# First-stage modulation of a two-layer diffusion trunk: a quarter of the columns to each column group of TensorE, instead of a quarter of the rows

## The chip, the cores and the metric

The kernel runs on one core of a Trainium2 chip. The metric is the device time of one execution in microseconds (us); the median of three runs before the change is 1126.43 us (1126.07 to 1126.88).

## What is computed

The reference is a trunk of two layers (DEPTH 2) over 256 latent and 256 context tokens of width 2048. Each layer first makes a shift, a scale and a gate from the conditioning vectors c and c_ctx, normalises the tokens, and multiplies the modulated tokens by a wide input matrix:

```
shift, scale, gate = split(silu(c) @ w_mod[l] + b_mod[l], 3)
shift_c, scale_c, gate_c = split(silu(c_ctx) @ w_mod[l] + b_mod[l], 3)
h   = rmsnorm(x,   g_pre[l]) * (1 + scale)   + shift
h_c = rmsnorm(ctx, g_pre[l]) * (1 + scale_c) + shift_c
proj = h @ w_in[l];  proj_c = h_c @ w_in[l]
```

Behind that come a gated position-mixing branch (columns a_u, a_v, a_g), windowed attention, a Fourier branch, and the output projection. The change touches only the making of shift and scale in layer 0.

## The kernel before, in words

Tokens lie transposed: 16 tiles `yo[k]` of 128 features by 512 tokens (256 latent, 256 context). All products with `w_in` and `w_out` are done on TensorE (PE) with each operand split into a high and a low part, three products per block: high by high, high by low, low by high. `hh[k]` and `hl[k]` are the two parts of tile k of the modulated input; `whi` and `wlo` those of the weights, made by ScalarE (ACT, the cast, L513) and VectorE (DVE, the subtraction, L515).

**The first stage** (the branch `if l == 0` of `layer`, L783 to L914) is a loop over the 16 feature tiles k, because the modulation of tile k+1 is finished only while tile k is being multiplied. In pass k of the loop, from k = 3 on, the order of PE is written by hand:

- `first_av` with (0,0) and (0,1): for four token blocks the products of `hh[k]` with the high and the low part of the a_v weights, 8 matmuls of 512 columns (L771, tile `ps_av`).
- `m.rounds()`: the modulation products of tile k+1 (L182, tile `ps_mod`). The weights of a tile are 16 row blocks (kk) of 128 rows by 256 columns (128 scale, 128 shift) in f32. The stationary operand is `cpad[:, kk]`, 128 by 32, of which two columns (c and c_ctx) are not zero. Row block kk goes to column group kk mod 4 of the array, so that each group of 32 output rows holds the sum over a quarter of the rows, for all 256 columns.
- `first_av` with (1,0): the products of `hl[k]`, 4 matmuls of 512 columns ("the low part").
- `m.cols()`: the second step. DVE has turned the 128 by 256 sums in blocks of 32 by 32 (`turn`, L188); four small matmuls with the 0/1 matrix `selq` (L194, tile `ps_modc`) add up the four column groups and put the result on the features' partitions.
- `start_au`: the products for three heads of a_u, 9 matmuls of 512 columns (L545 to L547, tile `ps_au`).

Each f32 matmul of the modulation is two instructions on PE, each with its own weight load. ACT turns the result of the second step into `gs` and `sh` (`mod_k`, L202, L203; for the first tiles DVE does, L205, L207), and `make_h1` makes the next tile: `hh[k+1]` by two ACT instructions of 256 columns (L663), the full-precision value by two more, then `hl[k+1]` by DVE (L665, `low_part`).

Two sets are special. Tile 10 (`Aside`) and the pair of tiles 14 and 15 (`AsidePair`, 512 columns at once) are summed in part on DVE (L231, L233): pieces of their weights are multiplied and added up in the passes that `SUMMED` lists (for the pair passes 9 to 12), at most `SLOT[k]` of these instructions between the turn of pass k and `low_part` (8 in passes 7, 8 and 12). PE multiplies only the rest of their row blocks and the two DVE sums (L242).

In this stage DVE, ACT and the queue of SyncE (SP), which issues the weight loads, run in the order in which the code is written. After it only PE does; DVE, ACT and SP are ordered by a scheduler at build time. The loads of a set go to fixed buffers, which are free once the set before last has been multiplied (`Mod.load`, L166 to L175). `splits(n)` emits the next cast and subtraction of `w_in` weights.

Of the kernel before, what the change touches and what calls it, by code (L numbers as in the profile page):

```python
# [13 lines left out]
P = 128  # L14
# [52 lines left out]
def trunk_kernel(ctx: ExitStack, tc: tile.TileContext, xT, xhalf, cT, wss, wsl, wmod, win, wout0, wout1, const, vec, rows,  # L67
# [91 lines left out]
    class Mod:  # L159
# [17 lines left out]
        def rounds(self, n=4):  # L177
            if self.ps is None:
                self.ps = ms_ps("mod")
            for kg in range(self.done, self.done + n):  # L180
                for kk in range(4):
                    PE.matmul(self.ps[32 * kk:32 * kk + 32, 0:self.N], cpad[:, kg * 4 + kk], self.w[kg * 4 + kk],  # L182
                              start=kg == 0, stop=kg == 3, tile_position=(0, 32 * kk))
            self.done += n

        def turn(self):
            self.r = w2k([P, self.N])
            V.transpose(self.r, self.ps[:, 0:self.N])  # L188

        def cols(self):  # L190
            ps = ms_ps("modc")
            rv = self.r.rearrange("p (j q c) -> p j q c", q=4, c=32)
            for q in range(4):
                PE.matmul(ps[32 * q:32 * q + 32, 0:4], cc("selq"), rv[:, :, q, 0:2], start=True, stop=True,  # L194
                          tile_position=(0, 32 * q))
            mod_k(self.k, ps[:, 0:4].rearrange("p (j s) -> p j s", s=2))

    def mod_k(k, v):

# [9 lines left out]
    class Aside(Mod):  # L209
# [25 lines left out]
        def rounds(self, n=4):  # L235
            n = 2 * sum(SUMMED[self.k].values())
            self.ps = ms_ps("mod")
            todo = [(cpad[:, kk], self.weights(kk)) for kk in range(n, KT)]
            todo += [(unit[:, s], self.sums(s)) for s in range(2)]
            for i, (st, mv) in enumerate(todo):  # L240
                c = slice(32 * (i % 4), 32 * (i % 4) + 32)
                PE.matmul(self.ps[c, 0:self.N], st, mv, start=i < 4, stop=i >= len(todo) - 4,  # L242
                          tile_position=(0, 32 * (i % 4)))

        def weights(self, kk):
            return self.w[kk // 2][:, kk % 2]
# [4 lines left out]
    class AsidePair(Aside):  # L251
# [17 lines left out]
            return self.acc[s]  # L269

        def cols(self):
            ps = ms_ps("modc")
            rv = self.r.rearrange("p (j q c) -> p j q c", q=4, c=32)
            for q in range(4):
                PE.matmul(ps[32 * q:32 * q + 32, 0:8], cc("selq"), rv[:, :, q, 0:2], start=True, stop=True,
                          tile_position=(0, 32 * q))
            v = ps[:, 0:8].rearrange("p (j k s) -> p j k s", k=2, s=2)
            mod_k(self.k, v[:, :, 0])
            self.second = lambda: mod_k(self.k + 1, v[:, :, 1])

# [443 lines left out]
    def layer(l):  # L724
# [58 lines left out]
        if l == 0:  # L783
            mod = {}
            for k in range(KT):
                def splits(n):
                    for _ in range(n):
                        W.emit()

                def next_h():  # L790
                    if k + 1 < KT:
                        if k < XAHEAD:
                            make_h0(k + 1)
                        else:
                            return make_h1(k + 1)
                    return lambda: None

                if k % 2 == 0:
                    take(k)
                if k == 0:  # L800
                    W.load()
                if k + 1 < KT and k + 1 not in (*LOADED, *(j + 1 for j in PAIRS)):
                    mod[k + 1] = Mod(k + 1)
                    mod[k + 1].load()
                if k < 2:
                    W.load_rest()
                for j, at in LOADED.items():
                    if j in PAIRS:
                        for _ in range(LOADS[k]):
                            W.load()  # L810
                    if k == min(at):
                        mod[j] = AsidePair(j) if j in PAIRS else Aside(j, "ctrh")
                    for _ in range(at.get(k, 0)):
                        mod[j].load_piece()

                def beside():
                    for j, at in SUMMED.items():
                        i = sum(at[i] for i in at if i < k)
                        for i in range(i, i + at.get(k, 0)):
                            yield from mod[j].steps(i)  # L820

                ops = beside()

                def aside(n):
                    for _ in range(n):
                        next(ops, None)

                m = mod.get(k + 1)
                if k == 0:
                    first_av(0, range(4), ((0, 0),))  # L830
                    first_av(0, range(4), ((0, 1),))
                    m.rounds(2)
                    first_av(0, range(4), ((1, 0),))
                    m.rounds(1)
                    e = W.emitting(512)
                    next(e)
                    next(e)
                    take(0, (1,))
                    m.rounds(1)
                    m.turn()  # L840
                    first_au(0, ((0, 0),))
                    next(state["e0"])
                    m.cols()
                    list(state["e0"])
                    first_au(0, ((0, 1),))
                    next_h()
                    state["e1"] = e
                elif k == 1:
                    first_au(0, ((1, 0),))
                    first_av(1, range(4), ((0, 0), (0, 1)))  # L850
                    m.rounds()
                    m.turn()
                    first_av(1, range(4), ((1, 0),))
                    m.cols()
                    e = W.emitting(512)
                    next(e)
                    start_au(1, (0, 1))
                    make_h0(2, e)
                    list(state["e1"])
                    list(e)  # L860
                    scale_x(3, rb0)
                elif k == 2:
                    first_av(2, range(4), ((0, 0),))
                    first_av(2, range(4), ((0, 1),))
                    first_av(2, range(4), ((1, 0),))
                    m.rounds()
                    m.turn()
                    start_au(2, (0,))
                    e = W.emitting(512)
                    next(e)  # L870
                    next(e)
                    m.cols()
                    start_au(2, (1,))
                    low_part = next_h()
                    scale_x(4, rb0)
                    scale_x(5, rb0)
                    low_part()
                    list(e)
                    ws_[2] = W.next()
                    for i in range(k + 1):  # L880
                        start_au(i, (2,))
                else:
                    pair = k + 1 in PAIRS
                    first_av(k, range(nt), ((0, 0), (0, 1)))
                    if m:
                        m.rounds()
                        m.turn()
                    if k < KT - 2:
                        splits(min(SPLITS[k], 1))
                    first_av(k, range(nt), ((1, 0),))  # L890
                    if m:
                        m.cols()
                    low_part = next_h()
                    if pair:
                        m.second()
                    aside(SLOT.get(k, 0))
                    for i in XSCALE.get(k, ()):
                        scale_x(i, rb0)
                    low_part()
                    if k == 4:  # L900
                        for i in (14, 15):
                            scale_x(i, rb0)
                    splits(SPLITS[k] if k >= KT - 2 else max(SPLITS[k] - 1, 0))
                    if k == KT - 2:
                        first_stage.close()
                    list(ops)
                    if k == KT - 3:
                        A.activation(sb([P, 4], F32, "es", 2), zero4, AF.Gelu_apprx_tanh)
                    if k >= KT - 2:
                        for _ in range(2):  # L910
                            with low(LAG), tc.issue_after(W.last.ins):
                                next(mods)
                    take(k, (1, 2))
                    start_au(k)  # L914
# [521 lines left out]
    with tc.manual_schedule(engines={EN.PE}):  # L1436
# [43 lines left out]
                PE.matmul(rb[:, j * P:(j + 1) * P], r0[:, j:j + 1].to_broadcast([P, P]), ident, start=True, stop=True)  # L1480

        m.rounds(1)
        m.turn()
        spread(0)
        scale_x(0, rb, LAT)
        m.cols()
        spread(1)
        rb0 = sb([P, T], F32, "acc")
        e = W.emitting(512)
        next(e)  # L1490
# [87 lines left out]
```

## Time and profile before

| | |
|---|---|
| median of 3 runs | 1126.43 us (1126.07 to 1126.88) |
| the profiled execution | 1126.57 us, of which the span from first to last instruction is 1124.8 us |
| PE busy | 1116.0 us, 99% of the span |
| DVE busy | 919.9 us, 82% |
| ACT busy | 548.8 us, 49% |
| loads on SP's queue | 229.79 MB |
| TensorE clock granted | 0.999 |

The profile is one execution, recorded on the chip. A matmul's end in it is modelled, so that a busy PE is not PE at its peak; what PE loses shows in the starts of its instructions. The chain of work is followed back from the last instruction: at each step to what released it, or to the instruction before it on its engine. PEld are the weight loads of PE, which can run beside its matmuls. In the lines of the timeline, the two numbers ahead are the start from the span's beginning and the length, in us; "x8" means that eight instructions of one kind are drawn together.

### The profile page before, as it was taken

Reading aid. Unit: us, or ns where it says so; the run is one execution under the profiler, and the core shown is the slowest. Engines: PE = TensorE matmul, PEld = TensorE weight load, DVE = VectorE, ACT = ScalarE, POOL = GpSimd, SP = SyncE. Lnnn points to the kernel's source line nnn. Section 1 sums busy time; section 2 is a strip of 40 time slices with the busy share of each in tenths; the row PEclk is TensorE's granted clock in tenths of the full one; section 3 lists DMA queues with packets and bytes.
Section 4 is the critical chain, followed back from the end, with each engine's and each line's share of the span. In section 5 each row is a group of like instructions: output and inputs, shape, how many; then the busy total and the mean of one; then the engine's idle time right before and its main releaser. Section 6 shows DMA issues by size and latency. Waiting matters only on the chain.

```text
span 1124.8 us, 16564 instructions
## 1 busy us (share of the span) xinstructions
PE 1116.0 (99%) x6069; PEld 919.4 (82%) x6072; DVE 919.9 (82%) x1573; ACT 548.8 (49%) x1044; POOL 34.9 (3%) x44
## 2 busy tenths in 40 slices
PE   8999999999999999999999999999999999999998
PEld 3666788888888888888888888988888888898886
DVE  2667699899988897988998989396989689878883
ACT  5454723322335667632533334266665369867551
POOL 0000000000000000000000000030500000000000
PEclk9999999999999999999999999999999999999999
DMA  9999755576655343465566665285946686456872
GB/s 360 402 401 399 258 165 173 168 241 206 212 189 182 112 152 121 128 202 186 169 194 206 218 207 186 95 197 193 236 154 204 211 294 198 159 180 200 302 254 75
DMA packets 76002, 235.84 MB, mean 210 GB/s; under 512 B 8704, under 2 KB 13200, under 8 KB 75920
## 3 DMA queue, kind: packets, MB, share of 16 engines
q1 hardware_dynamic: 71136, 229.79, 60.7%
q0 software_dynamic: 4064, 3.69, 2.2%
q10 hardware_dynamic: 720, 1.31, 0.3%
q8 instruction: 47, 0.77, 0.3%
q14 instruction: 35, 0.29, 0.1%
HBM read 232.65 MB, written 2.10 MB: 209 GB/s over the span
## 4 chain that ended last, share of the span: by engine, by line
PE 88%; DVE 5%; DMA 3%; ACT 2%; issue 1%; ACTq 0%; POOLq 0%; DVEq 0%; SPq 0%
PE ps_t L545 14%; PE ps_t L547 14%; PE ps_t L546 14%; PE ps_t L692 9%; PE ps_t L693 5%; PE ps_av L771 4%; PE ps_v L1174 3%; PE ps_y L545 3%; PE ps_y L547 3%; PE ps_y L546 3%; PE ps_mod L182 2%; DVE macc L294 2%; DVE wlo L515 1%; PE ps_v L1175 1%; PE ps_tp L1116 1%; DMA mraw<-in_wmod_dram 1%
## 5 line engine op out<-in xcount | busy, mean ns | idle before, releaser
L513 ACT CAST whi<-raw 128x1024 fp32r<-128x1024 f32 (+1 forms) x209 | 215.9, 1037 | 314.7 <-PE ps_t L546 214.0
L545 PE MATMUL ps_t<-hh,whi 128*128 128x512 f32 (+1 forms) x752 | 290.7, 387 | 0.0
L515 DVE TENSOR_TENSOR wlo<-raw,whi 128x1024 fp32r<-128x1024 f32 (+1 forms) x209 | 250.4, 1202 | 48.3 <-ACT whi L513 40.5
L546 PE MATMUL ps_t<-hl,whi 128*128 128x512 f32 (+1 forms) x752 | 289.6, 385 | 0.0
L547 PE MATMUL ps_t<-hh,wlo 128*128 128x512 f32 (+1 forms) x752 | 289.4, 385 | 0.0
L294 DVE SCALAR_TENSOR_TENSOR macc<-mraw,cs,macc 128x512 f32<-128x512 f32 x360 | 250.5, 744 | 14.6 <-DMA mraw<-in_wmod_dram 14.1
L692 PE MATMUL ps_t<-hh,whi 128*128 128x512 f32 x512 | 184.6, 399 | 0.0
L547 PEld LDWEIGHTS ps_t<-hh,wlo 128*128 128x128 f32 x752 | 141.3, 188 | 28.7
L545 PEld LDWEIGHTS ps_t<-hh,whi 128*128 128x128 f32 x752 | 141.3, 188 | 26.7
L546 PEld LDWEIGHTS ps_t<-hl,whi 128*128 128x128 f32 x752 | 141.3, 188 | 26.3
L693 PE MATMUL ps_t<-hh,wlo 128*128 128x256 f32 x512 | 143.4, 280 | 0.0
L692 PEld LDWEIGHTS ps_t<-hh,whi 128*128 128x128 f32 x512 | 96.1, 188 | 21.2
L693 PEld LDWEIGHTS ps_t<-hh,wlo 128*128 128x128 f32 x512 | 96.7, 189 | 0.4
L545 PE MATMUL ps_y<-whi,hh 128*128 128x512 f32 x104 | 41.3, 397 | 0.0
L547 PE MATMUL ps_y<-whi,hh 128*128 128x512 f32 x104 | 40.6, 391 | 0.0
L546 PE MATMUL ps_y<-wlo,hh 128*128 128x512 f32 x104 | 40.5, 389 | 0.0
L562 ACT CAST w2k<-ps_tp 128x512 fp32r<-128x512 f32 x40 | 23.4, 584 | 21.2 <-PE ps_scc L546 13.7
L575 POOL TENSOR_TENSOR rs_b<-rs_a,mhalf 128x2 f32<-128x2 f32 (+1 forms) x6 | 6.7, 1115 | 759.5 <-DVE mx L1366 584.6
L563 DVE TENSOR_TENSOR w2k<-ps_tp,w2k 128x512 fp32r<-128x512 f32 x40 | 27.4, 684 | 3.5 <-ACT w2k L562 2.3
L1096 ACT ACTIVATE w2k<-w2k,den 128x512 f32<-128x512 f32 (+1 forms) x48 | 28.1, 647 | 0.7 <-DVE den L1091 0.6
L188 DVE STREAM_TRANSPOSE w2k<-ps_mod 128x256 f32<-128x256 f32 (+1 forms) x15 | 7.0, 468 | 26.1 <-PE ps_mod L182 24.5
L771 PE MATMUL ps_av<-whi,hh 128*128 128x512 f32 x64 | 24.6, 397 | 0.0
(483 smaller groups left out, 1819.3 us busy)
## 6 DMA issues: line engine op xcount, KB each, us to landing
raw<-in_win_dram SPq DMA_DIRECT2D x158, 512.0 KB, 4.1
mraw<-in_wmod_dram SPq DMA_DIRECT2D x128, 512.0 KB, 4.4
raw<-in_wout_dram SPq DMA_DIRECT2D x60, 512.0 KB, 4.5
mraw<-in_wsl_dram SPq DMA_DIRECT2D x12, 512.0 KB, 7.3
mg<-in_wsl_dram SPq DMA_DIRECT2D x7, 512.0 KB, 9.0
mgl<-in_wsl_dram SPq DMA_DIRECT2D x7, 512.0 KB, 9.0
yo<-in_xhalf_dram POOLq DMA_DIRECT2D x28, 128.0 KB, 7.2
yo<-in_xT_dram SPq DMA_DIRECT2D x12, 256.0 KB, 4.9
```

Of the source, the lines that this page charges most:

```text
L294: V.scalar_tensor_tensor(out=acc[:, s], in0=w[:, kk % 2], scalar=c, in1=acc[:, s], op0=ALU.mult, op1=ALU.add)
L513: A.copy(ph, rc)
L515: self.last = V.tensor_tensor(out=pl, in0=rc, in1=ph.bitcast(F32), op=ALU.subtract)
L545: PE.matmul(ps, st[0], mv[0], start=start, stop=False)
L546: PE.matmul(ps, st[0], mv[1], start=False, stop=False)
L547: PE.matmul(ps, st[1], mv[0], start=False, stop=stop)
L563: V.tensor_tensor(out=lo, in0=src, in1=hi.bitcast(F32), op=ALU.subtract)
L692: PE.matmul(ps, w[0], h, start=k == 0, stop=False)
L693: PE.matmul(ps[:, 0:S], w[1], h[:, 0:S], start=False, stop=k == KT - 1)
L771: PE.matmul(ps, st[a], mv[b], start=start and (a, b) == (0, 0), stop=stop and (a, b) == (1, 0))
L1096: A.activation(prob[i][:, b * w:(b + 1) * w], prob[i][:, b * w:(b + 1) * w], AF.Copy, scale=den[:, c:c + 1])
L1174: PE.matmul(vps[t], hi, wk, start=k == 0, stop=False)
```

## The change

Column group q of the array now takes a quarter of the columns over all 16 row blocks. For each row block the same stationary operand is loaded into all four groups, and each group multiplies 64 columns: two runs of 32 (one of scale, one of shift). The sums are then complete, and the turn of the 128 by 64 result (128 by 128 for the pair) puts them on the features' partitions. The second step with `selq` is gone; `mod_k` reads the turned tile in SBUF instead of PSUM. In passes k >= 3 the modulation's products and the turn stand behind the low part of a_v, so that the subtraction of `splits` stands ahead of the turn in DVE's order. Ahead of the loop, the two halves of `spread` (the broadcast of the first norm's factors) stand together ahead of the turn, and the second step's matmuls no longer stand between them.

```diff
@@ class Mod
             for kg in range(self.done, self.done + n):
-                for kk in range(4):
-                    PE.matmul(self.ps[32 * kk:32 * kk + 32, 0:self.N], cpad[:, kg * 4 + kk], self.w[kg * 4 + kk],
-                              start=kg == 0, stop=kg == 3, tile_position=(0, 32 * kk))
+                for kk in range(4 * kg, 4 * kg + 4):
+                    self.row(cpad[:, kk], self.w[kk], kk == 0, kk == KT - 1)
             self.done += n
 
+        def row(self, st, mv, start, stop):
+            mv = mv.rearrange("p (j q c) -> p j q c", q=4, c=32)
+            for q in range(4):
+                PE.matmul(self.ps[32 * q:32 * q + 32, 0:self.N // 4], st, mv[:, :, q], start=start, stop=stop,
+                          tile_position=(0, 32 * q))
+
         def turn(self):
-            self.r = w2k([P, self.N])
-            V.transpose(self.r, self.ps[:, 0:self.N])
+            self.r = w2k([P, self.N // 4])
+            V.transpose(self.r, self.ps[:, 0:self.N // 4])
 
         def cols(self):
-            ps = ms_ps("modc")
-            rv = self.r.rearrange("p (j q c) -> p j q c", q=4, c=32)
-            for q in range(4):
-                PE.matmul(ps[32 * q:32 * q + 32, 0:4], cc("selq"), rv[:, :, q, 0:2], start=True, stop=True,
-                          tile_position=(0, 32 * q))
-            mod_k(self.k, ps[:, 0:4].rearrange("p (j s) -> p j s", s=2))
+            mod_k(self.k, self.r.rearrange("p (j c) -> p j c", c=32)[:, :, 0:2])
@@ class Aside, rounds (the same in AsidePair.cols: no matmuls, r read directly)
             for i, (st, mv) in enumerate(todo):
-                c = slice(32 * (i % 4), 32 * (i % 4) + 32)
-                PE.matmul(self.ps[c, 0:self.N], st, mv, start=i < 4, stop=i >= len(todo) - 4,
-                          tile_position=(0, 32 * (i % 4)))
+                self.row(st, mv, i == 0, i == len(todo) - 1)
@@ layer, passes k >= 3
                     first_av(k, range(nt), ((0, 0), (0, 1)))
-                    if m:
-                        m.rounds()
-                        m.turn()
                     if k < KT - 2:
                         splits(min(SPLITS[k], 1))
                     first_av(k, range(nt), ((1, 0),))
                     if m:
+                        m.rounds()
+                        m.turn()
                         m.cols()
@@ ahead of layer(0)
         m.rounds(1)
+        spread(0)
+        spread(1)
         m.turn()
-        spread(0)
+        m.cols()
         scale_x(0, rb, LAT)
-        m.cols()
-        spread(1)
```

More of the change, by code (lines that the diff above doesn't have):

```diff
@@ L271, in cols @@
         def cols(self):
[L272 to L277, printed above, removed]
+            v = self.r.rearrange("p (j k c) -> p j k c", k=2, c=32)[:, :, :, 0:2]
             mod_k(self.k, v[:, :, 0])
```

## The prediction, made before the changed kernel ran

> **What bounds the kernel now.** I read the page first, then the busy time by stage, then the chain of work through the first stage.
>
> ```profile
> PE 1116.0 (99%) x6069; PEld 919.4 (82%) x6072; DVE 919.9 (82%) x1573; ACT 548.8 (49%) x1044; POOL 34.9 (3%) x44
> ...
> DMA  9999755576655343465566665285946686456872
> ...
> q8 instruction: 47, 0.77, 0.3%
> ```
>
> PE is busy 99% of the span, and the DMA engines are full in the first four of the 40 slices (112 us), not later. The view of busy time by stage, for passes 3, 12 and 13 of the first stage (pass 13 multiplies the pair):
>
> ```profile
> 45.81:53.07 7.26, 7.26 (x62) 4.88 (x62) 4.64 (x8) 3.53 (x8) 0.00 (x0) 1.00 1.03 398
> ...
> 109.95:117.22 7.27, 7.27 (x63) 4.88 (x62) 6.12 (x10) 3.53 (x8) 0.00 (x0) 1.00 1.05 392
> 117.22:124.50 7.28, 7.28 (x47) 4.39 (x46) 4.63 (x7) 3.53 (x8) 0.00 (x0) 1.00 0.62 233
> ```
>
> A pass takes 7.27 us, all of it PE. (The columns are PE, PEld, DVE, ACT and POOL with their instructions, then PE's clock, the DMA engines' share and GB/s.) Two others are close behind: the loads, with a share of 1.03 to 1.05, and in pass 12 DVE with 6.12 us. The chain of work through passes 12 and 13:
>
> ```profile
> 109.95 1.82 PE ps_av L771 x8
> 111.77 1.86 PE ps_mod L182 x32
> 113.63 1.13 PE ps_av L771 x4
> 114.76 0.17 PE ps_modc L194 x8
> 114.94 0.43 PE ps_au L545
> 115.36 0.23 PE ps_au L546
> ...
> 117.22 1.82 PE ps_av L771 x8
> 119.04 1.85 PE ps_mod L242 x16
> ...
> 122.04 0.18 PE ps_modc L275 x8
> 122.22 0.43 PE ps_au L545
> ...
> 124.50 0.70 PE ps_av L771 x3
> ```
>
> No gap: in the first stage the end is set by PE's program, and what PE saves there counts as long as loads, ACT and DVE keep up. A matmul of 512 columns costs 0.23; the first behind a change of the array's division costs 0.43.
>
> **The change, step by step.** *The second step goes.* 0.17 us, and since the low part now follows the high part without a change between, its four cost 4 x 0.23 = 0.93 instead of 1.13. That is 0.37 us a pass. What hid the turn's latency was the low part; what is late next is weighed below.
>
> *The products.* 32 instructions of 256 columns become 128 of 64, each with its own weight load. The timeline of pass 3:
>
> ```profile
> 48.44 0.61 PE L182 MATMUL ps_mod<-macc,kt 128*32 128x256 f32 x8
> 48.87 0.61 PE L182 MATMUL ps_mod<-vv,kt 128*32 128x256 f32 x8
> 49.42 1.20 PE L771 MATMUL ps_av<-whi,hl 128*128 128x512 f32 x4
> 50.54 0.24 PE L194 MATMUL ps_modc<-w2k,cst 128*32 128x4 f32 x8
> 50.72 0.50 PE L545 MATMUL ps_au<-hh,whi 128*128 128x512 f32 x1
> ```
>
> Eight start within 48.87 - 48.44 = 0.43 us: four groups at once, 0.215 us a round. A quarter of the columns is 0.054 a round, and 32 rounds give the same 1.72 as 8 rounds before. So the columns cost nothing more; the question is whether PE starts 256 instructions (loads counted) in that time, 7 ns each. The nearest row: the 16 of the second step (8 loads, 8 matmuls of four columns, where columns cost next to nothing) take 50.72 - 50.54 = 0.18 us, 11 ns each, and that with the change of division in it. The ends are thus +0 and 256 x 11 ns = 2.8 us, +0.95 on 1.86. Less than +0 is excluded, the columns being the same. I take +0.09, near the lower end, since in the rows above weight loads run beside matmuls without lengthening a round.
>
> [...]
>
> A full pass then gives 0.37 - 0.09 = 0.28 us.
>
> *The way from the products to `hh[k+1]`.* It is now covered by a_u alone: 0.43 + 8 x 0.23 = 2.3 us. ACT in pass 4, then DVE:
>
> ```profile
> 58.12 0.35 ACT L202 ACTIVATE gs<-ps_modc,gg,vecs 128x2 f32<-128x2 f32 x1 [3.70 <-PE ps_modc L194]
> 58.66 1.09 ACT L663 ACTIVATE hh<-yo,sh,gs 128x256 fp32r<-128x256 f32 x2
> 59.66 1.08 ACT L663 ACTIVATE w2k<-yo,sh,gs 128x256 f32<-128x256 f32 x2
> ```
> ```profile
> 49.55 0.45 DVE L188 STREAM_TRANSPOSE w2k<-ps_mod 128x256 f32<-128x256 f32 x1 [2.62 <-PE ps_mod L182]
> ...
> 60.78 0.69 DVE L665 TENSOR_TENSOR hl<-w2k,hh 128x512 fp32r<-128x512 f32 x1 [1.10 <-ACT w2k L663]
> ...
> 80.10 1.66 DVE L233 SCALAR_TENSOR_TENSOR ctrh<-kt,cs,ctrh 128x256 f32<-128x256 f32 x4
> ...
> 83.26 0.69 DVE L665 TENSOR_TENSOR hl<-w2k,hh 128x512 fp32r<-128x512 f32 x1
> ...
> 113.70 0.45 DVE L188 STREAM_TRANSPOSE w2k<-ps_mod 128x256 f32<-128x256 f32 x1 [0.48 <-PE ps_mod L182]
> 114.07 0.71 DVE L233 SCALAR_TENSOR_TENSOR nstrh<-yo,cs,nstrh 128x512 f32<-128x512 f32 x1
> ...
> 119.34 0.69 DVE L665 TENSOR_TENSOR hl<-w2k,hh 128x512 fp32r<-128x512 f32 x1
> ...
> 121.04 0.72 DVE L188 STREAM_TRANSPOSE w2k<-ps_mod 128x512 f32<-128x512 f32 x1 [1.02 <-PE ps_mod L242]
> ```
>
> Call E the end of the last product (48.87 + 0.61 = 49.48 in pass 3). The turn starts at E + 0.07. 256 columns take 0.45 and 512 take 0.72, so 64 take about 0.25: done at E + 0.32. `gs` starts 0.04 later, `hh` 0.54 behind it (58.12 to 58.66), its first half is there at E + 1.5. PE wants it at E + 2.1. Hidden, with 0.6 to spare; that also covers `mod_k`, whose reading from SBUF no row shows (its rows from PSUM are 0.35 and 0.25, and half as much more would not be seen).
>
> *The low part comes 1.9 us earlier in a pass*, and it needs `hl`. In before the products stood ahead of it. PE asks for `hl[k+1]` at E + 2.1 + 8 x 0.23 = E + 4.0. By ACT's rows it is ready at E + 0.36 + (61.47 - 58.12) = E + 3.7: just in time. But where DVE has its sums between turn and `hl`, they decide. Passes 7 and 8: eight sums of 0.395 (80.10 to 83.26), ready at E + 0.07 + 0.19 + 3.16 + 0.69 = E + 4.1; with the 0.1 to 0.2 that a stop of PE costs, 0.3 each. **Pass 12**: eight sums of 0.66 (114.07 to 119.34), so E + 0.07 + 0.19 + 5.27 + 0.69 = E + 6.2 against E + 4.0. PE stands 2.2 us, 2.3 with the restart, ahead of the low part of pass 13. Before, the pair's products filled that time (119.04 + 1.85 = 120.9, `hl` there at 120.03). The pair's products, which wait for the same sums, now come behind low part and all: passes 12 and 13 together take 14.55 - 2 x 0.28 + 2.3 = 16.3 us.
>
> *Loads.* SP issues as the DMA engines take them, 400 GB/s throughout:
>
> ```profile
> DMA packets 14663, 39.21 MB, mean 400 GB/s; under 512 B 1628, under 2 KB 1628, under 8 KB 14653
> ```
> ```profile
> L174 SPq DMA_DIRECT2D yo<-in_wsl_dram x4: 328/328/328, 74.5 to 77.7; - x4
> ...
> DMA to landing us min/median/max: 7.2/7.5/8.4
> ```
> ```profile
> 83.95 1.86 PE ps_mod L182 x32
> ```
>
> They don't get faster. The last weights of pass 8 land at 77.7 + 7.2 = 84.9; PE's products there end at 83.95 + 1.86 = 85.8, and the quarter that needs these weights begins some 0.6 before, at 85.2. The products now stand 0.9 us later in the pass and take their row blocks in order, which gives 0.3 more: PE may come 1.5 us earlier (1.8 with the stop ahead of it) and no more. Buffers come free 0.9 us later, against 7 us between issue and landing: no effect on the rate.
>
> *The start and the rest.* In passes 0 to 2 the loads set the pace, and only the second steps of passes 1 and 2 count, less 0.2 for `hh[2]`, which ACT makes behind a cast that waits for its load: 0.55. Pass 3 loses 0.1, since the subtraction, late there for the same reason, is now ahead of the turn.
>
> **The sum**, against the profiled 1126.57: start 0.55; passes 3 to 8, 10 and 11, eight x 0.28 = 2.24; pass 9 (a short set) 0.35; less 0.1, less 0.6; gives 2.44 gained at pass 12. Passes 12 and 13 lose 16.3 - 14.55 = 1.75. Left: 0.7, so 1125.9. Behind the stage I count nothing: PE runs there without gaps in a fixed order. The scheduler may order DVE and ACT otherwise; the trace has no price for it, and 0.5 is my choice for the likeliest value, against the gain, since an order with no gaps can only get some: 1126.4.
>
> **The rivals.**
>
> *Starts of instructions set the pace* (slower). Beyond 7 ns each nanosecond costs 0.26 us a set, 2.8 us in eleven sets, so that it decides from 8 ns on. At 11 ns a set takes 2.8 us and a pass loses 0.57 instead of gaining 0.28: eight passes 4.6; the start 0.8 (two sets of 0.85 more, 0.4 of it beside waits for loads, less the 0.55); pass 9 nothing; stops 0.7; passes 12 and 13 1.75 + 0.85: +8.7, 1135. For it: the 11 ns. Against: that row has a change of division in it. [...]
>
> *Late code blocks* (slower). PE's 6069 + 6072 instructions came in 47 packets of the instruction queue, 258 to a packet of 16 KB. A pass had 62 + 62 (row of pass 3) and now has 124 - 64 - 16 + 256 = 300, so a block is used up in 6 us, and when it falls on the products alone, in under 3. A fetch must pass DMA engines that are full, where data takes 7 us to land. Two or three late ones of 1 us: 1129.
> [...]
>
> *`hl` isn't late* (faster). If the pass-12 stop doesn't come, the whole 2.44 + 0.6 + 0.56 stands, cut by the loads to 1.5 at pass 8 and then 0.28 + 0.35 + 4 x 0.28, about 3.2: 1123.3. Against: DVE's order is written out, and its rows are plain.
>
> **How the numbers follow.** Forecast, 1126.4 with its own range 1124.8 to 1128: 0.58. Starts: 0.18. Code blocks: 0.16. `hl` in time: 0.08. A measurement tells 0.2% (2.25 us) from no change. Faster than 1124.2: the last, 0.08. Slower than 1128.7: the starts, and two thirds of the blocks, and a scheduler's mishap: 0.31. Range: 1124.5 to 1131, leaving out 0.05 below and the starts' 0.15 above.
>
> **What would show it.** A full pass of 6.99 us; rounds of the products 0.054 to 0.06 apart; no `ps_modc`; in passes 8 and 9 short waits of PE for `hl` (DVE L665), in pass 13 one of 2.2 us; the pair's products starting near 119.6 instead of 119.0, and a_u of pass 13 within 1 us of 122.2. It is wrong if the products take over 2.2 us, if PE stands with nothing that the profile shows, or if gaps come up behind 134 us.

## The result, and the profile after

| | before | after |
|---|---|---|
| median | 1126.36 us (1126.07 to 1126.88, 4 runs) | 1139.33 us (1136.55 to 1141.67, 4 runs) |
| profiled execution, its span | 1126.57, 1124.8 us | 1136.55, 1134.8 us |
| end of the first stage (first `ps_t`) | 133.94 us | 143.61 us |

The changed kernel is slower by about 1%: ratio 1.0114, 95% interval 1.0091 to 1.0137. The profiled execution is the fastest of its four. Of the 10.0 us between the two spans, 9.7 are there at the end of the first stage. The page of the changed kernel:

```profile
PE 1114.0 (98%) x7269; PEld 932.8 (82%) x7272; DVE 917.2 (81%) x1573; ACT 550.2 (48%) x1044; POOL 34.9 (3%) x44
```

PE has 2 us less to do (1114.0 against 1116.0) and takes 10 us longer. The busy sums even point the wrong way; what grew is idle time. The busy time by stage of two undisturbed full passes, and of passes 12 and 13 together:

```profile
47.36:54.27 6.91, 6.91 (x151) 5.70 (x150) 4.22 (x8) 2.92 (x6) 0.00 (x0) 1.00 1.04 395
54.27:61.22 6.95, 6.95 (x150) 5.62 (x150) 4.55 (x8) 3.60 (x8) 0.00 (x0) 1.00 1.04 408
...
117.20:134.09 16.89, 14.50 (x236) 11.39 (x235) 7.84 (x13) 5.42 (x12) 0.00 (x0) 1.00 0.55 186
```

(In both kernels a window's count can take in a matmul of its neighbour: a full pass of the changed kernel has 149 matmuls.) So a pass does get shorter, 7.27 to 6.95 us, a little more than forecast (6.99). The chain of work through passes 7 and 8 shows what takes it back:

```profile
50.08 1.92 PE ps_mod L188 x128
...
75.12 0.68 PE ps_av L764 x3
75.80 0.41 issue
76.21 2.37 PE ps_av L764 x9
78.57 1.81 PE ps_mod L188 x118
80.38 2.54 issue
82.92 0.59 PE ps_mod L188 x10
...
84.23 0.43 PE ps_au L539
...
87.05 2.74 PE ps_av L764 x12
...
94.00 3.04 PE ps_av L764 x12
```

A set of 128 products takes 1.92 us where nothing disturbs it. In pass 7 PE stops twice, once in the middle of a row of products and once in the middle of a_v, and waits for nothing that the profile shows ("issue"); behind the longer stop a matmul of 512 columns costs 0.43 in place of 0.23. From 75.12 to 87.05 the pass takes 11.93 us. PE's timeline has all such stops of the first stage; the bracket is the idle time ahead of the instruction and who ended it:

```profile
36.34 0.24 PE L188 MATMUL ps_mod<-vv,kt 128*32 128x64 f32 x1 [2.36 <-issue]
...
76.21 0.50 PE L764 MATMUL ps_av<-wlo,hh 128*128 128x512 f32 x1 [0.41 <-issue]
82.92 0.59 PE L188 MATMUL ps_mod<-vv,kt 128*32 128x64 f32 x10 [2.54 <-issue]
...
115.05 0.39 PE L538 MATMUL ps_au<-hh,whi 128*128 128x512 f32 x1 [3.47 <-issue]
...
121.97 0.53 PE L188 MATMUL ps_mod<-yo,kt 128*32 128x64 f32 x21 [0.27 <-issue]
...
128.73 1.20 PE L764 MATMUL ps_av<-whi,hl 128*128 128x512 f32 x4 [2.13 <-DVE hl L658]
```

Five stops without a reason, 2.36 + 0.41 + 2.54 + 3.47 + 0.27 = 9.05 us. The sixth is the wait for `hl` in pass 13, forecast at 2.2 us. The granted clock behind the stop at 80 us (the last three columns are the granted clock, the DMA share and GB/s):

```profile
82.80:84.00 1.20, 1.08 (x11) 0.84 (x11) 0.46 (x2) 0.17 (x1) 0.00 (x0) 0.51 1.06 382
84.00:86.20 2.20, 2.20 (x7) 1.69 (x6) 2.20 (x7) 2.17 (x6) 0.00 (x0) 0.50 1.02 386
```

By the clock records of the trace it is half from 82.83 us on, for 3.41 us. Half the clock for 3.4 us costs another 3.4 / 2 = 1.7. Now take the stages that lie between the starts behind these stops, and add up matmuls and weight loads (the columns with x):

```profile
36.30:75.60 39.30, 39.26 (x765) 31.85 (x765) 24.36 (x45) 20.12 (x40) 0.00 (x0) 1.00 1.03 401
75.60:80.60 5.00, 4.37 (x128) 3.32 (x128) 1.92 (x2) 1.22 (x2) 0.00 (x0) 1.00 1.04 406
82.80:111.90 29.10, 28.66 (x510) 22.78 (x510) 20.03 (x42) 13.53 (x28) 0.00 (x0) 0.94 0.94 350
115.00:121.60 6.60, 6.55 (x128) 5.34 (x127) 2.22 (x3) 0.54 (x1) 0.00 (x0) 1.00 1.04 382
```

1530, 256, 1020 and 255: six, one, four and one times 256, but for a few records at the windows' edges or missing. Counting every record of PE, with the semaphore instructions of its sequencer, from the start of the trace is sharper: 960, 2496, 2751, 3775 and 4032 lie ahead of the five stops, which leaves 192, 192, 191, 191 and 192 over a multiple of 256. The wait for `hl` leaves 12. PE stops at the borders of blocks of 256 instructions, though not at all of them. The DMA queue of instructions has one packet in the stretch from 80.3 to 81.5 us, in the longer stop of pass 7, and none from there to 82.9:

```profile
q8 instruction: 1, 0.02, 5.8%
```

PE starts again at 82.92, which is 1.45 us behind the end of this packet; at the other four stops it starts 1.33 to 1.38 behind the end of one (by the packets' own times in the trace). For the whole first stage the same queue has, after and then before:

```profile
q8 instruction: 17, 0.28, 0.8%
```
```profile
q8 instruction: 7, 0.11, 0.4%
```

**The theory (A)**, an inference from these counts: the next block of instructions is fetched only when PE enters the one ahead of it (each of the 17 packets begins 1.6 to 4.6 us behind the first instruction of a block, by the packets' times and the count of records), and when a block is used up before the fetch is done, PE stands. The 42 instructions of a_v and a_u in a pass take 5 us, the 256 of products 1.9. With about one semaphore instruction a pass has 299, so that a border falls some 43 instructions earlier in each pass than in the one before it, and a block is late only where it holds little but products. It is left open whether a fetch always takes that long (A1) or because the DMA engines are full (A2). **The rivals**: the new order of a pass makes PE stop (B), or the new layout does, a column group over all rows with one stationary operand (C).

### The profile page after: what moved, and what is told of

Its sections match the earlier page's. It is cut to its first block, busy times and chain, and to the rows that moved or that the text cites. A ratio compares the mean times of both kernels' runs of the same rounds, so it can differ in the third digit from the quotient of the medians.

```text
span 1134.8 us, 18964 instructions
## 1 busy us (share of the span) xinstructions
PE 1114.0 (98%) x7269; PEld 932.8 (82%) x7272; DVE 917.2 (81%) x1573; ACT 550.2 (48%) x1044; POOL 34.9 (3%) x44
## 4 chain that ended last, share of the span: by engine, by line
PE 90%; DVE 3%; DMA 3%; ACT 3%; issue 1%; ACTq 0%; POOLq 0%; DVEq 0%; SPq 0%
PE ps_t L538 15%; PE ps_t L539 15%; PE ps_t L540 15%; PE ps_t L685 9%; PE ps_t L686 5%; PE ps_av L764 3%; PE ps_v L1166 3%; PE ps_y L538 3%; PE ps_y L540 3%; PE ps_y L539 3%; PE ps_mod L188 2%; PE ps_v L1167 1%; PE ps_tp L1108 1%; DMA vv<-in_wsl_dram 1%; PE ps_au L538 1%
## 5 line engine op out<-in xcount | busy, mean ns | idle before, releaser
L193 DVE STREAM_TRANSPOSE w2k<-ps_mod 128x64 f32<-128x64 f32 (+1 forms) x15 | 3.8, 255 | 37.3 <-PE ps_mod L188 37.3
L556 DVE TENSOR_TENSOR w2k<-ps_tp,w2k 128x512 fp32r<-128x512 f32 x40 | 27.4, 685 | 3.8 <-ACT w2k L555 2.6
L202 ACT ACTIVATE gs<-w2k,gg,vecs 128x2 f32<-128x2 f32 x13 | 5.0, 386 | 48.2 <-DVE w2k L193 48.2
```

The costliest lines, as they stand in the source:

```text
L556: V.tensor_tensor(out=lo, in0=src, in1=hi.bitcast(F32), op=ALU.subtract)
```

## The experiments

**1. More instructions, nothing else** (`e1_quarters`): the kernel before, each product cut into four pieces.

```diff
-                for kk in range(4):
-                    PE.matmul(self.ps[32 * kk:32 * kk + 32, 0:self.N], cpad[:, kg * 4 + kk], self.w[kg * 4 + kk],
-                              start=kg == 0, stop=kg == 3, tile_position=(0, 32 * kk))
+                for q in range(4):
+                    for kk in range(4):
+                        c = slice(64 * q, 64 * q + 64)
+                        PE.matmul(self.ps[32 * kk:32 * kk + 32, c], cpad[:, kg * 4 + kk], self.w[kg * 4 + kk][:, c],
+                                  start=kg == q == 0, stop=kg == q == 3, tile_position=(0, 32 * kk))
```

> The kernel before, with each product of the modulation (L182) cut into four pieces of 64 columns: row blocks, column groups, order, second step and loads stay, a set has 256 instructions on PE instead of 64. Theory A (code blocks: PE's program comes in blocks of 256 instructions, the next is asked for when one is used up, and the fetch is slow while the DMA engines are full): 1131 to 1141 us, with two to five gaps of PE of 1 to 4 us that no wait explains, each ending over a us behind the end of an instruction-queue packet. Theory B (the new order: products, turn and freed buffers 0.9 us later): 1126 to 1128 us, no such gap. Theory C (four groups on one row block and one stationary operand): 1126 to 1128 us, no such gap.

Measured: 1138.51 us, ratio 1.0099 (1.0082 to 1.0116). PE's timeline and chain of this kernel:

```profile
30.81 0.23 PE L196 MATMUL ps_modc<-w2k,cst 128*32 128x4 f32 x5 [1.10 <-issue]
...
38.85 0.49 PE L184 MATMUL ps_mod<-vv,kt 128*32 128x64 f32 x18 [2.93 <-issue]
```
```profile
61.50 1.93 PE ps_mod L184 x128
...
70.63 2.11 issue
```

The old layout in the old order, with the second step and without any wait for `hl`, loses 12.0 us, nearly as much as the change (13.0). There are three stops, 6.1 us in all, and each ends 1.33 to 1.39 us behind the end of an instruction packet, as expected. The number of instructions is enough; B and C are not needed for it. An undisturbed set costs 1.93 here, 0.07 more than before.

**2. The old place in the pass** (`e2_old_place`): the changed kernel, products and turn ahead of the low part again.

```diff
                     first_av(k, range(nt), ((0, 0), (0, 1)))
+                    if m:
+                        m.rounds()
+                        m.turn()
                     if k < KT - 2:
                         splits(min(SPLITS[k], 1))
                     first_av(k, range(nt), ((1, 0),))
                     if m:
-                        m.rounds()
-                        m.turn()
                         m.cols()
```

> The changed kernel with the products and the turn of passes k >= 3 back ahead of the low part of a_v. Theory A: gaps as in the changed kernel, 1129 to 1138 us; the wait of 2.1 us for hl in pass 13 is gone. Theory B: 1124 to 1126 us, no gaps. Theory C: gaps as in the changed kernel, 1129 to 1138 us.

Measured: 1135.45 us, ratio 1.0076 (1.006 to 1.0091), 3.9 less than the change. The wait for `hl` is gone. The chain keeps three of the stops, against B (A and C both expected that):

```profile
34.07 2.37 issue
78.93 2.73 issue
111.12 2.29 issue
```

**3. Fewer sums on DVE in pass 12** (`e6_fewer_sums`): the changed kernel with four sums there in place of eight.

```diff
-    SUMMED = {10: {5: 1, 6: 1, 7: 3, 8: 2}, 14: {9: 1, 10: 1, 11: 1, 12: 2}}
+    SUMMED = {10: {5: 1, 6: 1, 7: 3, 8: 2}, 14: {9: 1, 10: 1, 11: 1, 12: 1}}
```

> The changed kernel with four DVE sums in pass 12 instead of eight (PE multiplies ten row blocks of the pair instead of eight of its own work: two more, 0.44 us). If the wait of 2.1 us in pass 13 is DVE's order, as the prediction has it, that wait is gone and the changed kernel's time falls by 1.5 to 2 us, to 1136 to 1139; its gaps at block ends stay. If the pair's loads were behind the wait, it stays.

Measured: 1137.51 us, ratio 1.009 (1.0073 to 1.0106): 1.8 less than the change, as expected, though the runs of the two kernels overlap (up to 1137.98 here, from 1136.55 there). What decides is the trace: the wait in pass 13 isn't there. That wait was the price of the new place, as forecast, but it is the small part of the loss.

**4. Half of the loads** (`e3_half_loads`, and `e4_before_half_loads` with the same edit in the kernel before).

```diff
-                    DMA.dma_start(w, wsl[ALONE.index(k), kg][:, kk:kk + step])
-                    self.w += [w[:, i] for i in range(step)]
+                    h = step // 2
+                    DMA.dma_start(w[:, 0:h], wsl[ALONE.index(k), kg][:, kk:kk + h])
+                    self.w += [w[:, i % h] for i in range(step)]
```

> The changed kernel with half of each modulation weight load of the single tiles left out (two row blocks share one buffer half, so the modulation is not the reference's); instructions of PE and their order stay, the DMA engines have room. Theory A: the gaps fall from 9.7 us in all to under 2 us, and the time is within 3 us of the control e4. Theory C: the gaps stay at 8 to 11 us, e4 plus 8 to 13. Theory B (late loads) expects them gone too, so this run tells A from C only.

> Control for e3: the kernel before with the same half of the modulation weight loads left out (the modulation is not the reference's). All theories: 1120 to 1125 us, since passes 0 to 2 no longer wait for loads; passes from 3 on keep their 7.27 us.

Measured: 1137.81 us (1.0099, 1.0075 to 1.0123) and 1124.93 us (0.9984, 0.9975 to 0.9994). The control has no stops. In the changed kernel those near 34 and 75 us are gone, but the two longest stay (3.80 and 3.02 us, and 0.34 behind them); busy time by stage, then PE's timeline:

```profile
76.00:80.00 4.00, 4.00 (x129) 3.24 (x128) 1.92 (x2) 1.34 (x2) 0.00 (x0) 1.00 0.85 266
```
```profile
83.97 0.58 PE L189 MATMUL ps_mod<-vv,kt 128*32 128x64 f32 x10 [3.80 <-issue]
```

Here my expectation failed. I had taken it that half the loads would make the fetch quick; the DMA engines were still busy 85% of the time ahead of the longest stop. By its time alone, 12.9 us above the control, this run came out as theory C expected; so it doesn't tell A from C, and what stands against C is experiment 1, with the old layout.

**5. A quarter of the loads** (`e7_quarter_loads`).

```diff
-            for kg in range(4):
+            for kg in range(1):
...
+            self.w = self.w * 4
```

> The changed kernel with three quarters of the modulation weight loads of the single tiles left out (every set multiplies its first four row blocks four times, so the modulation is not the reference's); PE's instructions and order stay. Theory A1 (a fetch takes about 5 us whatever the loads): gaps at the block ends as before, 1 to 4 us each, 1130 to 1138 us. Theory A2 (it is slow because the DMA engines are full): the gaps fall to under 2 us in all, 1122 to 1127 us.

Measured: 1130.78 us, ratio 1.0038 (1.0024 to 1.0052), its runs spread from 1127.1 to 1135.1. The profiled one is the fastest of the ten, 1127.09, so that its trace doesn't show what the others lost. In it one unexplained stop of length is left, behind a stretch in which the engines' share was again 0.82:

```profile
106.47 0.40 PE L539 MATMUL ps_au<-hh,whi 128*128 128x512 f32 x1 [2.32 <-issue]
```
```profile
97.00:104.00 7.00, 7.00 (x162) 5.67 (x150) 4.79 (x7) 3.59 (x7) 0.00 (x0) 1.00 0.82 272
```

That is neither A1 (gaps as before) nor A2 (under 2 us in all), but it has fewer stops with fewer loads: loads seem to make the fetch longer. How long it is without any, this kernel doesn't tell.

**6. A third as many instructions more** (`e5_halves`): as `e1_quarters`, in two pieces of 128 columns.

> The kernel before, with each product of the modulation cut into two pieces of 128 columns: 128 instructions a set, some 188 a pass instead of 124; columns, order and second step stay. Theory A, in its form after the first runs (a block of 256 instructions must last over 5 us, else PE waits): a block lasts at least 1.9 us for the products and 128 of the slower instructions beside them, over 9 us, so no gaps and 1126 to 1128 us. A rival by which more and smaller instructions themselves cost (start rate, PSUM) would give a third of what quarters gave, 1129 to 1132 us.

Measured: 1128.41 us, ratio 1.0016 (1.0007 to 1.0025), and no stop in the first stage that the trace puts down to nothing. A set of 128 instructions lasts 1.88 us here, one of 256 in `e1_quarters` 1.93, with 6.1 us of stops. So the stops don't grow in proportion with the instructions; they come when a block gets too short. The time lies between the two expectations, 0.4 above A's 1128 and 0.6 below the rival's 1129. Where the 1.8 us of this kernel come from was not followed up (0.7 are there at the end of the first stage), so that a small price of the instructions themselves is not ruled out.

**7. The fetch by itself** (`e8_bursts`): the kernel before, with 1280 small PE instructions in a row at three places.

```diff
+    def burst(ps, n):
+        for i in range(n):
+            c = slice(32 * (i % 4), 32 * (i % 4) + 32)
+            PE.matmul(ps[c, 0:64], ones[:, 0:32], ones[:, 0:64], start=True, stop=True, tile_position=(0, 32 * (i % 4)))
...
+                    if k == 6:
+                        burst(ms_ps("burst"), 320)
...
+        finish()
+        burst(mm_ps("burst"), 320)
...
+        if l == 0:
+            burst(mm_ps("burst"), 320)
```

> The kernel before with three bursts of 320 small products (64 columns, four column groups, 1280 instructions or five blocks each, a result that nobody reads): behind pass 6 while the loads are full, ahead of the four cg tiles of layer 0 while they are about half, and behind everything else. Without fetches a burst is 80 rounds of 2 x 0.06 = 9.6 us. Theory A1: 20 to 30 us for each burst, with a gap every 256 instructions. Theory A2: 20 to 30 us for the first, under 14 us for the last, the second between. Theory C or a limit on starts: no gaps at 256, the three of one length.

Measured: 1177.12 us, a single run. PE's timeline of the burst in the first stage and of the one at the end (each row is a run of instructions without a stop):

```profile
81.34 3.52 PE L595 MATMUL ps_burst<-ones 128*32 128x64 f32 x128 [3.65 <-issue]
87.81 3.52 PE L595 MATMUL ps_burst<-ones 128*32 128x64 f32 x128 [2.95 <-issue]
91.82 1.99 PE L595 MATMUL ps_burst<-ones 128*32 128x64 f32 x128 [0.48 <-issue]
```
```profile
1161.85 1.99 PE L595 MATMUL ps_burst<-ones 128*32 128x64 f32 x128 [1.07 <-issue]
1165.31 1.99 PE L595 MATMUL ps_burst<-ones 128*32 128x64 f32 x128 [1.47 <-issue]
1168.77 1.99 PE L595 MATMUL ps_burst<-ones 128*32 128x64 f32 x128 [1.47 <-issue]
```

This is the clearest picture of the study. Each run is 128 matmuls, with their loads 256 instructions, and between two runs PE always stops. From start to start a block takes 87.81 - 81.34 = 6.47 us in the one case and 1165.31 - 1161.85 = 3.46 in the other (then 3.46 and 3.73), though its instructions need 1.99, or 3.52 at half the clock. The DMA share in these stretches (last column but one):

```profile
81.30:87.70 6.40, 3.52 (x128) 3.35 (x128) 0.00 (x0) 0.00 (x0) 0.00 (x0) 0.74 1.05 390
87.70:91.70 4.00, 3.52 (x128) 3.28 (x128) 0.00 (x0) 0.00 (x0) 0.00 (x0) 0.57 0.54 194
...
1165.20:1168.70 3.50, 1.99 (x128) 1.84 (x128) 0.00 (x0) 0.00 (x0) 0.00 (x0) 1.00 0.02 5
```

A block costs 3.45 to 3.73 us on engines that are nearly empty (five blocks in the three bursts, share 0.02 to 0.09). With a share of 0.54 one took 4.0, and one in the burst in the middle, at 0.55, took 4.55; the one with full engines (1.05) took 6.5. So a fetch has neither one length whatever the loads, nor a length that comes from the loads alone: some 3.5 us are its own, and full engines add to them. The bursts took 22, 17 and 16 us, so that A1 and A2 each missed a part; C expected no stops at every 256th instruction.

What full engines add isn't one figure. At the five stops of the changed kernel PE goes on 5.2 to 6.9 us after the first instruction of the block ahead (256 records back), with the DMA share at 1.02 to 1.05 in between. The packet itself takes 1.0 to 1.1 us, and PE goes on 1.3 to 1.5 us behind its end; it is the start of the packet that comes 2.7 to 4.6 us after that first instruction, against 1.0 to 1.3 on the nearly empty engines at the end of `e8_bursts`. At late borders in the first stage of the other kernels the whole takes from 4.4 us (`e7_quarter_loads`, 102.1 to 106.47, behind a share of 0.82) to 8.3 (`e11_old_place_shift136`, 58.39 to 66.71).

**8. Moving the borders** (`e9_shift136`, `e10_shift208`, `e11_old_place_shift136`): 136 or 208 more PE instructions ahead of everything, in the time in which PE waits for its first input (74 or 110 small matmuls, two instructions each, for six large ones); the third kernel has the edit of experiment 2 as well. (Theory R: the stops belong to certain passes, not to a count.)

```diff
-                warm(idle, 3 if k else 6)
+                if k:
+                    warm(idle, 3)
+                else:
+                    for _ in range(74):
+                        PE.matmul(idle[:, 0:64], wz[:, 0:P], wz[:, 0:64], start=True, stop=True)
```

> The changed kernel with 136 more PE instructions ahead of everything: the six idle matmuls of 512 columns, in the time in which PE waits for its first input, become 74 of 64 columns (148 instructions in place of 12). Nothing else is changed. Theory A (a block of 256 instructions is fetched only when PE enters the block ahead of it, and that takes 5 to 6 us): the borders of the blocks move 136 instructions forward, so the gaps leave 33.8, 75.4, 80.2, 111.4 and 121.5 us and come where the borders now fall on a set of products. With one fetch of 5.2 to 6.0 us per block, worked out over PE's starts in the trace of the changed kernel, that is 51.5 (1.4 to 2.2 us) and 57.5 to 59 (0.5 to 1.3 us), none at 34, 75, 80 or 121: some 2 to 3.5 us in place of 9.5, no halved clock, 1128 to 1131 us. Theory R (the gaps belong to those passes, by their loads or by what PE waits for there, and not to a count): they stay within 2 us of where they were, and 1137 to 1139 us.

> The same with 208 more instructions in place of 136 (110 small idle matmuls). Theory A: gaps at 41.1 (3.3 to 4.1 us), 88.5 (1.9 to 2.7) and 121 to 123 (2.4 to 3.2), and none near 34, 75, 80 and 111: 7.5 to 10 us, with the clock halved behind the longest, so 1135 to 1140 us. Theory R: gaps where the changed kernel has them, and 1137 to 1139 us.

> Both together: products and turn back ahead of the low part (as in e2_old_place, without its wait for hl in pass 13) and 136 more instructions at the start. Theory A: gaps at 51.3 (0.8 to 1.6 us) and 56 to 57.5 (1.2 to 2.0), 2 to 3.6 us in all in place of 7.8, so e2_old_place's 1135.5 less 4 to 6 us and less the halved clock's 1 to 2: 1128 to 1130 us. If the column groups' saving of the second step (0.17 to 0.3 us a pass) came through whole, it would stand at 1126, level with the kernel before. Theory R: 1135 us as in e2_old_place.

Measured, against 1127.01 of the kernel before: 1132.14 us (1.0056, 1.0035 to 1.0076), 1135.70 (1.0075, 1.006 to 1.009) and 1128.18 (1.0015, 1.0005 to 1.0024). From the chains of the three, in this order:

```profile
52.52 0.51 issue
57.93 3.23 issue
```
```profile
91.22 1.88 issue
122.35 1.91 issue
```
```profile
56.13 2.26 issue
65.24 1.47 issue
```

With 136 more instructions the stops at 34, 75, 80 and 111 us are gone, and there are two near 52 and 58, where the borders were worked out to fall. With 208 more they are near 91 and 122 (88.5 and 121 to 123 were worked out), and a third at 43.2 to 46.5 (41.1 worked out), which the view puts down mostly to ACT's `hh`. The count puts it among the borders: 1473 records lie ahead of it, 193 over a multiple of 256. The ten kernels with such stops have 39 of over 0.2 us in the first stage and the bursts, this one included, and every one of them leaves 190 to 194; the stops that a wait for data or for another engine explains leave anything from 11 to 213. No load and no product was changed in experiment 8, so theory R falls. The working by one constant fetch was not good for sizes: at 58 us 0.5 to 1.3 were expected and 3.23 came (that fetch took 8.1 us, not 5.2 to 6.0), with the clock halved behind it, so that `e9_shift136` missed its 1128 to 1131; `e10_shift208` is within its 1135 to 1140; and in `e11_old_place_shift136` the stops came a block later than worked out, though their sum (3.7 us) was about as expected. That kernel, within its 1128 to 1130, is the best of the changed ones and still not ahead of the kernel before. Without its two stops it would stand at 1128.2 - 3.7 = 1124.5 by the median, or at 1130.0 - 3.7 = 1126.3 by the profiled execution, which is among the slowest of its ten; these are estimates that no run bears out: no layout without a stop was found. The profiled execution has lost something else too: the first stage ends at 134.07 us, level with 133.94 before, but the rest of the span takes 994.1 us in place of 990.9, of which 1.1 is a wait of PE for DVE (`mgl`, L556). The rest was not followed up.

## Why the prediction was wrong

**The failed step is the rival "Late code blocks".** Its mechanism was named, with its chance at 0.16, and it is the one that happened; its price was wrong, and the sum of the forecast itself has no term for it. The rival took "two or three late ones of 1 us", 1129. The runs show five, of up to 3.47 us, 9.05 in all, and 1.7 for the halved clock, of which the prediction says nothing. The price could have been worked out better from rows that stood in it: under 3 us for a block of products, against 7 us that data took to land through the same full engines, leaves 4 us for a block that is late, not 1. And the drift of the border, 300 - 256 = 44 instructions a pass by the counts that it gave (43 by the trace), brings it back to the same place about every sixth pass. Two or three stops of up to 4 us would have been 8 to 12 us, an estimate made with hindsight, and the range would have had to reach it. The sign that the prediction gave for it, PE standing with nothing that the profile shows, is what was seen.

The other steps, in their order:

- *The start*, 0.55 us: without its stop of 2.36, pass 3 begins at 45.00 us instead of 45.81, so 0.8.
- *The second step and the change of division*, 0.37 us a pass, and *the products*, +0.09: right, and a little better together. A pass lasts 6.95 us, a set 1.92 (1.95 forecast).
- *Starts of instructions set the pace*: refuted. 128 matmuls in 1.92 us are 15 ns each, with their loads 7.5 ns an instruction.
- *The way to `hh[k+1]`*: hidden, as said. The turn of 64 columns takes the 0.25 us that were worked out.
- *Loads*: not put to the test. PE has no wait for them from pass 3 on, but the stops kept it later than the forecast had it.
- *`hl` in pass 13*: right in place, cause and size. PE waited 2.13 us for it (2.2 forecast), and DVE's order is the one that was argued. Passes 12 and 13 together take 16.89 us, 0.27 of it a stop (16.3 forecast):

```profile
122.55 0.25 DVE L193 STREAM_TRANSPOSE w2k<-ps_mod 128x64 f32<-128x64 f32 x1 [5.08 <-PE ps_mod L188]
122.72 0.71 DVE L233 SCALAR_TENSOR_TENSOR nstrh<-yo,cs,nstrh 128x512 f32<-128x512 f32 x1
...
127.99 0.69 DVE L658 TENSOR_TENSOR hl<-w2k,hh 128x512 fp32r<-128x512 f32 x1
```

- *Short waits for `hl` in passes 8 and 9*: seen in pass 9, in place and size. Its 12 matmuls of a_v take 3.04 us from 94.00 on, those of pass 8 2.74; DVE ends `hl` at 95.77, and the low part starts at 95.83 instead of 95.67; of the 0.30 that the pass loses by it, 0.16 are this wait and 0.14 the stop itself. Pass 8 has no such wait: the halved clock had drawn out a_u ahead of it, so that PE came later.
- *Behind the stage nothing*: right for this kernel, 0.3 us of the 10.0 lie there. In other runs it isn't so little: 2.4 us more than before in `e6_fewer_sums`, 3.3 in `e11_old_place_shift136`.

The sum without the blocks was 1125.9 to 1126.4. With 9.05 and 1.7 it gives 1136.7 to 1137.2; the profiled execution took 1136.55. That nothing else is missing is shown by this sum only, and for this execution only; that the blocks are the cause is shown by experiments 1, 7 and 8 and by the count of records. A set of products uses up 256 instructions in 1.92 us, 7.5 ns each, against 3.45 us and more for a block in `e8_bursts`.

## What to carry to other kernels

Count instructions as well as columns. In these kernels PE stopped at borders of 256 instructions, weight loads among them, where a block was used up sooner than the next one came: 3.45 to 3.73 us a block with the DMA engines nearly empty (`e8_bursts`), 4.4 to 8.3 at the late borders of the first stage. It isn't the mean that counts but the shortest stretch that a border can fall on (here a set of products, 1.92 us), and the border moves from pass to pass by the pass's count modulo 256 (here some 43). Such a stop, which ends in "issue", was recognised here by counting PE's records from one to the next, which gave multiples of 256 within a few records, and tested by putting 136 or 208 instructions ahead of everything, which moved the stops.

## What the runs showed of the hardware that was not expected

- **A fetch of instructions has a length of its own**, 3.45 to 3.73 us a block with the DMA share at 0.02 to 0.09 (`e8_bursts`). Most of it is not the bytes: 16 KB pass in one packet, in the changed kernel 5.8% of 16 engines' time in the 1.2 us from 80.3 on, which is 1.1 us of one engine.
- **The clock is halved after stops as short as 1.9 us, but not after all.** In the changed kernel it was halved behind the stop of 2.54 us and stayed at 1.00 behind those of 2.36 and 3.47 us:

```profile
36.30:39.70 3.40, 3.35 (x15) 2.74 (x16) 2.93 (x8) 2.13 (x4) 0.00 (x0) 1.00 1.05 397
```
```profile
115.00:118.40 3.40, 3.35 (x15) 2.75 (x15) 2.22 (x3) 0.54 (x1) 0.00 (x0) 1.00 1.04 380
```

  In `e10_shift208` it was halved behind both of 1.9 (and behind that at 43 us), by the stages:

```profile
94.40:97.80 3.40, 3.40 (x10) 2.62 (x9) 3.40 (x9) 2.97 (x5) 0.00 (x0) 0.50 1.01 340
...
125.10:128.40 3.30, 3.30 (x9) 2.56 (x8) 3.30 (x5) 0.34 (x1) 0.00 (x0) 0.50 0.02 6
```

  These two halved stretches last some 3.4 us by the windows, the one of the changed kernel 3.41 by its clock records. So the length of a stop alone doesn't tell whether the clock is halved behind it. What does was not shown, and how much idleness is enough was not tried.
- **The time of a kernel with late blocks spreads**: 1136.6 to 1141.7 us over four runs of the changed kernel, against 1126.1 to 1126.9 of the kernel before. The three runs without a trace are 2.7 to 5.1 us longer than the profiled one, at a granted clock of 0.994 to 0.995 in place of 0.998. That lower clock is worth 3 to 5 us over the span, an estimate that fits more halved stretches, which no trace shows.
